# A hybrid RG-LRU and latent-attention trunk on one core: first weight chunks in one transfer, the first sums behind nine products, the last stage's sums on rounded parts

## The chip, the cores and the metric

The kernel runs on one core of a Trainium2 chip. The metric is device time in microseconds (us), the median of several runs; lower is better. The engines are TensorE (PE in the profile; PEld is its weight load), VectorE (DVE), ScalarE (ACT), GpSimd (POOL) and SyncE (SP), which here only issues transfers. Each engine works through its own list of instructions in the order in which they were written or scheduled, and they meet through semaphores.

## The reference

One sequence of 1024 positions with 1024 channels passes through a recurrent layer and then through an attention layer that reads one shared set of keys and values; a last RMS norm ends it.

```
h  = rms_norm(x, norm_a);  u = h @ w_in_a             # 1024 -> 2 x 1280
xb = causal_conv4(u[:, :1280]) ; gate = u[:, 1280:]
r, i = sigmoid(xb @ w_rg + b_rg), sigmoid(xb @ w_ig + b_ig)   # ten blocks of 128
a  = exp(-8 r softplus(-lam));  hs = scan(a, sqrt(1 - a^2) * i * xb)
x  = x + (hs * silu(gate)) @ w_out_a
ckv, k_rope from rms_norm(x, norm_kv) @ w_dkv;  k, v from rms_norm(ckv)
u  = rms_norm(x, norm_b) @ w_in_b;  q from rms_norm(u[:, :384]);  gate = u[:, 384:]
o  = causal attention of 8 heads (scores over 128 + 64 channels)
x  = x + (o * silu(gate)) @ w_out_b
out = rms_norm(x, final_norm)
```

## The kernel before

Channels lie on the 128 partitions and the 1024 positions along the free dimension; a tile of 512 positions is a half, `hs(0)` or `hs(1)`. A float32 number is kept as two parts in the type F32R: `hi`, a rounded copy that ScalarE makes, and `lo`, the rest, that VectorE makes by a subtraction (`hl`). A product is then three matmuls, hi by hi, hi by lo and lo by hi (`mm3`, lines 117 to 119).

**The beginning** (lines 286 to 365) is written out by hand for SP, ACT and DVE (`manual_schedule`); the lists of the other engines, and of all engines in the rest of the program, come from the scheduler. `warm` is nine matmuls on ones, whose results nobody reads. ACT issues the two transfers with the first 128 columns of the first x-branch chunk (`wx`) and gate chunk (`wg`) of the input weights. SP issues x (`xload`, tile by tile of 128 channels), with the remaining weights in between; ahead of them all it issues `vec`, a small table of gains and biases. `xsplit(k)` multiplies tile k of x by the norm's gain from `vec` and splits it into parts: ACT makes hi (L255), DVE lo (L256). The products start with the tiles k = 0 and 1, half by half (`first`, L325), and go on tile by tile (`products`), 96 matmuls for four accumulators `ps0`. In between ACT squares x (L278, L280) and DVE adds the squares into `accp` (L150, L152), since the norm's factor is applied to the results and not to x. The factor needs the sum over the partitions: `accp` is split into `ap`, and per half two matmuls with a matrix of ones (`onesr`, L362) give the sum; then `newton` makes the reciprocal square root with two ACT and two DVE instructions (L142 to L145) into `rb`.

**The loop over the ten chunks** `ct` follows. For a chunk, `conv` scales the products by `rb` (`byr`, L156), runs the convolution on DVE (L384) and splits the result `xc` (L85 on ACT, L86 on DVE); `rgig` multiplies the split result by the two gate matrices, six matmuls per half; and the products of the next chunk (`psn`, 48 matmuls on `wx`) and of its gate (`pg1` for chunk 1, 24 per half) stand ahead of `rgig` on PE. Weights of later chunks come as a raw float32 copy on SP and a rounded copy on POOL; DVE subtracts one from the other (L101). The softplus of `lam` is some 45 instructions of ten columns (`sp`), spread over DVE's list.

**The last stage** (lines 1043 to 1140) is the output product and the final norm. The first half of the positions goes tile by tile (eight tiles `dt`), the squares are added into `acc`; in the second half five tiles are 512 wide, and three are cut into two quarters, `qa` and `qb_`, of 256. Each norm sums its squares over the partitions with a float32 matmul on ones: `acc` at L1125, the first quarter's `acc2` at L1134, the second's at L1112 and L1113. `root` runs `newton`, and `multiplies` scales the tiles and issues the stores.

Of the kernel before, what the change touches and what calls it, by code (L numbers as in the profile page):

```python
# [10 lines left out]
F32R = mybir.dt.float32r  # L11
# [38 lines left out]
NWARM = 9  # L50
# [10 lines left out]
def trunk(tc, xT, wina, vecs, wgate, wouta, winc, wuk, wuv, wuq, wuqr, woutb, rope, outT):  # L61
# [69 lines left out]
    nc.sync.dma_start(out=vec, in_=vecs)  # L131
# [158 lines left out]
    with tc.manual_schedule(engines={_E.SP, _E.Activation, _E.DVE}):  # L290
        w0 = [Weights(wina[j][:, 0:4 * P], w) for j, w in ((0, wx), (NCT, wg))]
        for w in w0:
            w.load(0, 1, nc.scalar)
# [7 lines left out]
        xload(0, hs(0))  # L301
        xload(0, hs(1))
# [5 lines left out]
        xload(3)  # L308
        step(SPN[0])
        w0[0].split(0, 1)  # L310
        w0[1].split(0, 1)
        xsplit(0, hs(0))
# [43 lines left out]
        for h in range(2):  # L356
            hl(accp[:, hs(h)], *ap[h])
        for h in range(2):
            t1, t2 = tt(), tt()
            ps = pst()  # L360
            for i in range(2):
                T.matmul(out=ps, lhsT=onesr, rhs=ap[h][i], start=i == 0, stop=i == 1)  # L362
            newton(rb[:, hs(h)], ps, 1.0 / D, t1, t2)
# [79 lines left out]
    for ct in range(NCT):  # L443
# [12 lines left out]
        if ct + 1 < NCT:  # L456
            wg = wtile(wina[NCT + ct + 1], NKT, cast=True)
            psn = [pst(), pst()]
            for h in range(2):
                mmt(psn[h], wx, xs, hs(h))  # L460
            if ct == 0:
                pg1 = [pst(), pst()]
                for h in range(PG1):
                    mmt(pg1[h], wg, xs, hs(h))
            prev = (ct, rgig(ct, ws, xcs), gt)
            if ct == 0:
                for h in range(PG1, 2):
                    mmt(pg1[h], wg, xs, hs(h))
# [579 lines left out]

    def products(dt, c, po, k0=0, mid=None):
        k1 = NKT if mid is None else 5  # L1050
        mmt(po, wob[dt][k0:k1], ysb[k0:k1], c, first=k0 == 0, last=k1 == NKT)
        if mid:
            mid()
            mmt(po, wob[dt][k1:], ysb[k1:], c, first=False)
# [6 lines left out]
    for dt in range(NKT):  # L1061
# [14 lines left out]
        x2s.append(x2)  # L1076

# [42 lines left out]
    for dt in range(NWIDE):  # L1120
        tile2(dt, slice(0, HW))
        if dt == 1:

            ps = pm()
            T.matmul(out=ps, lhsT=onesd, rhs=acc, start=True, stop=True)  # L1125
# [4 lines left out]
    for dt in range(NWIDE, NKT):  # L1130
        tile2(dt, qa)
    def norm():
        ps = pm()[:, 0:HW // 2]
        T.matmul(out=ps, lhsT=onesd, rhs=acc2[:, qa], start=True, stop=True)  # L1134
        root(HW // 2, ps, acc2[:, qa])

    tile2(NWIDE, qb_, norm)
    multiplies(QUARTER, qa)
    for dt in range(NWIDE + 1, NKT):
        tile2(dt, qb_)  # L1140
    multiplies(FINAL, qb_)
# [54 lines left out]
```

## Time and profile before

| | |
|---|---|
| median of three runs | 866.5 us (866.46 to 866.98) |
| the profiled execution, its own time | 866.23 us |
| its span, first to last instruction | 864.5 us |
| mean granted clock of TensorE | 0.996 |
| busy, share of the span | PE 99%, DVE 76%, ACT 60%, POOL 9% |

The profiled execution's own time is 1.73 us above its span, and 0.27 us below the median. A busy share says how long an engine had an instruction in it; what an instruction waited for stands in the view of waits and, in brackets, at the end of a row of the timeline. Matmuls are pipelined: one lasts longer in the profile than the time from its start to that of the next.

### The profile page before, as it was taken

How to read it: one execution, taken by the hardware profiler on the slowest of the kernel's cores; microseconds unless marked ns; L12 is line 12 of the kernel's file. 1: busy time of each engine (PE TensorE's matmuls, PEld its weight loads, DVE VectorE, ACT ScalarE, POOL GpSimd, SP SyncE). 2: the span in 40 equal slices, each digit the busy share in tenths (PEclk: the TensorE clock that was granted, in tenths of full speed). 3: DMA queues.
4: the chain of work that ended last, by engine and by line, in shares of the span. 5: the costliest groups of instructions: out<-in, count | busy, mean ns of one | idle time of the engine just before them, and what ended most of it. 6: DMA issues, size and time to landing. Idle time of an engine off the chain costs nothing.

```text
span 864.5 us, 11922 instructions
## 1 busy us (share of the span) xinstructions
PE 851.9 (99%) x4206; PEld 721.7 (83%) x4206; DVE 659.5 (76%) x1216; ACT 519.9 (60%) x959; POOL 73.6 (9%) x143
## 2 busy tenths in 40 slices
PE   8999999999999999999999999999999999999995
PEld 6788888888888888888888889888998998888885
DVE  7888778777877773779998957887797887875254
ACT  8557787777688542699976555555565564431132
POOL 1000110110000110100312320000000000010000
PEclk9999999999999999999999999999999999999998
DMA  8333333333213445123545674122231323867022
GB/s 300 92 98 98 98 97 99 107 95 98 79 43 92 151 144 184 51 98 121 170 147 202 213 252 125 53 91 83 77 113 62 105 82 132 335 211 247 0 98 98
DMA packets 51052, 108.98 MB, mean 126 GB/s; under 512 B 6448, under 2 KB 15024, under 8 KB 50992
## 3 DMA queue, kind: packets, MB, share of 16 engines
q1 hardware_dynamic: 34928, 67.05, 23.7%
q0 software_dynamic: 15216, 40.51, 14.1%
q8 instruction: 33, 0.54, 0.3%
q10 hardware_dynamic: 848, 0.66, 0.2%
q14 instruction: 27, 0.22, 0.1%
HBM read 81.46 MB, written 26.21 MB: 125 GB/s over the span
## 4 chain that ended last, share of the span: by engine, by line
PE 95%; DVE 2%; issue 1%; DMA 1%; ACT 1%; SPq 0%; DVEq 0%
PE ps L118 18%; PE ps L117 18%; PE ps L119 18%; PE pm L119 6%; PE pm L117 6%; PE pm L118 6%; PE pm L922 4%; PE pm L938 2%; PE pm L939 2%; PE s L905 2%; PE s L903 2%; PE s L904 2%; PE s L906 2%; PE s L902 2%; PE pm L937 2%
## 5 line engine op out<-in xcount | busy, mean ns | idle before, releaser
L118 PE MATMUL ps<-pg,wh 128*128 128x512 f32 x664 | 258.7, 390 | 0.6 <-DVE pg L256 0.5
L119 PE MATMUL ps<-pg,wl 128*128 128x512 f32 x664 | 258.4, 389 | 0.0
L117 PE MATMUL ps<-pg,wh 128*128 128x512 f32 x664 | 257.8, 389 | 0.0
L118 PEld LDWEIGHTS ps<-pg,wh 128*128 128x128 f32 x664 | 124.6, 188 | 27.7 <-DVE pg L256 2.1
L117 PEld LDWEIGHTS ps<-pg,wh 128*128 128x128 f32 x664 | 124.6, 188 | 26.3 <-DVE tk L657 0.3
L119 PEld LDWEIGHTS ps<-pg,wl 128*128 128x128 f32 x664 | 124.6, 188 | 25.7
L85 ACT ACTIVATE pt<-pm 128x512 fp32r<-128x512 f32 (+2 forms) x96 | 44.4, 490 | 58.1 <-PE pm L922 54.8
L912 ACT ACTIVATE pg<-s,m 128x128 f32<-128x128 f32 (+3 forms) x64 | 47.5, 743 | 47.1 <-DVE m L909 40.7
L117 PE MATMUL pm<-pg,pg 128*128 128x512 f32 (+1 forms) x152 | 54.9, 361 | 0.0
L118 PE MATMUL pm<-pg,pg 128*128 128x512 f32 (+1 forms) x152 | 54.5, 359 | 0.0
L119 PE MATMUL pm<-pg,pg 128*128 128x512 f32 (+1 forms) x152 | 54.3, 357 | 0.0
L86 DVE TENSOR_TENSOR pt<-pm,pt 128x512 fp32r<-128x512 f32 (+2 forms) x96 | 50.5, 549 | 3.2 <-ACT pt L85 3.2
L909 DVE TENSOR_REDUCE m<-s 128x1 f32<-128x128 f32 (+3 forms) x64 | 48.1, 753 | 1.2
L384 DVE SCALAR_TENSOR_TENSOR t<-xb,vec,t 128x512 f32<-128x512 f32 x60 | 44.8, 746 | 0.4
L85 ACT ACTIVATE wh<-wr 128x512 fp32r<-128x512 f32 (+3 forms) x55 | 29.1, 531 | 25.4 <-PE ps L118 12.9
L85 ACT ACTIVATE pg<-pg 128x512 fp32r<-128x512 f32 x42 | 26.1, 631 | 29.5 <-DVE pg L438 18.1
L86 DVE TENSOR_TENSOR wl<-wr,wh 128x512 fp32r<-128x512 f32 (+3 forms) x55 | 30.6, 566 | 15.5 <-ACT wh L85 15.3
L119 PE MATMUL pm<-pg,wl 128*128 128x512 f32 x108 | 42.4, 392 | 0.0
L922 PE MATMUL pm<-ident,pg 128*128 128x128 f32 x288 | 42.3, 274 | 0.0
L118 PE MATMUL pm<-pg,wh 128*128 128x512 f32 x108 | 42.3, 392 | 0.0
L117 PE MATMUL pm<-pg,wh 128*128 128x512 f32 x108 | 42.2, 390 | 0.0
L902 PE MATMUL s<-pg,pg 128*128 128x512 f32 (+2 forms) x96 | 37.0, 386 | 0.4 <-ACT pg L912 0.4
(238 smaller groups left out, 1782.1 us busy)
## 6 DMA issues: line engine op xcount, KB each, us to landing
wr<-wina SPq DMA_DIRECT2D x38, 256.0 KB, 2.8
wh<-wina POOLq DMA_DIRECT2D x36, 256.0 KB, 2.9
wa<-winc SPq DMA_DIRECT2D x24, 256.0 KB, 3.2
ysd<-pg POOLq DMA_DIRECT2D x12, 512.0 KB, 3.0
pg<-ysd SPq DMA_DIRECT2D x12, 512.0 KB, 10.6
wr<-wouta SPq DMA_DIRECT2D x16, 256.0 KB, 2.7
t<-xT SPq DMA_DIRECT2D x16, 256.0 KB, 3.6
x1d<-t POOLq DMA_DIRECT2D x16, 256.0 KB, 2.5
```

The costliest lines, as they stand in the source:

```text
L85: A.activation(out=hi, in_=src, func=AF.Copy)
L86: V.tensor_tensor(out=lo, in0=src, in1=f(hi), op=ALU.subtract)
L117: T.matmul(out=ps, lhsT=w[0], rhs=r[0], start=first, stop=False, skip_group_check=more)
L118: T.matmul(out=ps, lhsT=w[0], rhs=r[1], start=False, stop=False, skip_group_check=more)
L119: T.matmul(out=ps, lhsT=w[1], rhs=r[0], start=False, stop=last, skip_group_check=more)
L384: V.scalar_tensor_tensor(out=xc, in0=xb[:, j:j + HW], scalar=cwv[j], in1=xc, op0=ALU.mult, op1=ALU.add)
L902: T.matmul(out=sc[:, c], lhsT=q[0][:, ql], rhs=k[0][:, c], start=True, stop=False)
L903: T.matmul(out=sc[:, c], lhsT=q[0][:, ql], rhs=k[1][:, c], start=False, stop=False)
L904: T.matmul(out=sc[:, c], lhsT=q[1][:, ql], rhs=k[0][:, c], start=False, stop=False)
L909: V.tensor_reduce(out=m, in_=sc, axis=AX.X, op=ALU.max, negate=True)
L912: A.activation(out=p_[:, 0:nk], in_=sc, func=AF.Exp, bias=m, accum_out=l)
L922: T.transpose(out=ps[:, (b - b0) * P:(b - b0 + 1) * P], in_=p_[:, b * P:(b + 1) * P], identity=ident)
```

## The change

Five edits:

- The two first weight chunks come in one transfer on ACT's queue, of 128 partitions by 2 by 128 columns, into one tile `raw0`; the rounding of both (`hl`) reads from there and stands ahead of the first five instructions of the softplus.
- SP issues the first half of x tile 0 ahead of `vec`. `warm` has eight matmuls instead of nine.
- Nine products of the next chunk (`psn0`: tiles k = 0 to 2 of the first half) stand ahead of the first sums (L362) in the program; the loop's first pass then takes k = 3 to 7 for this half.
- The sums of `acc` and of the first quarter's `acc2` in the last stage are made of the two rounded parts, as the first sums are: `sumparts` splits, and `total` is two F32R matmuls in place of one float32 matmul. The one of `acc2` stands behind seven of the eight k of its tile, instead of five.
- The last of the first quarter's four scalings with its store stands behind the next tile's product.

```diff
-NWARM = 9
+NWARM = 8
...
     vec = con.tile([P, NVEC], F32, name="vec")
-    nc.sync.dma_start(out=vec, in_=vecs)
...
-        for w in w0:
-            w.load(0, 1, nc.scalar)
+
+        raw0 = tt()[:, 0:2 * P]
+        nc.scalar.dma_start(out=raw0.rearrange("p (j c) -> p j c", c=P), in_=wina[0:NCT + 1:NCT, :, 0:P].rearrange("j p c -> p j c"))
...
         xload(0, hs(0))
+        nc.sync.dma_start(out=vec, in_=vecs)
         xload(0, hs(1))
...
+        for i, w in enumerate(w0):
+            hl(raw0[:, i * P:(i + 1) * P], w.hi[:, 0:P], w.lo[:, 0:P])
+        xsplit(0, hs(0))
         step(SPN[0])
-        w0[0].split(0, 1)
-        w0[1].split(0, 1)
-        xsplit(0, hs(0))
         xsplit(0, hs(1))
...
             hl(accp[:, hs(h)], *ap[h])
+        psn0 = pst()
+        mmt(psn0, wx[:3], xs[:3], hs(0), last=False)
         for h in range(2):
             t1, t2 = tt(), tt()
...
-            psn = [pst(), pst()]
+            psn = [psn0 if ct == 0 else pst(), pst()]
             for h in range(2):
-                mmt(psn[h], wx, xs, hs(h))
+                k0 = 3 if (ct, h) == (0, 0) else 0
+                mmt(psn[h], wx[k0:], xs[k0:], hs(h), first=k0 == 0)
...
+    def sumparts(a):
+
+        n = a.shape[-1]
+        p_ = td.tile([P, n], F32R, tag="t1", name=nm("t1")), td.tile([P, n], F32R, tag="t2", name=nm("t2"))
+        hl(a, *p_)
+        return p_
+
+    def total(ps, p_):
+
+        for i in range(2):
+            T.matmul(out=ps, lhsT=onesr, rhs=p_[i], start=i == 0, stop=i == 1)
+
     def products(dt, c, po, k0=0, mid=None):
-        k1 = NKT if mid is None else 5
+        k1 = NKT if mid is None else 7
...
         x2s.append(x2)
+    ap = sumparts(acc)
...
-            T.matmul(out=ps, lhsT=onesd, rhs=acc, start=True, stop=True)
+            total(ps, ap)
             root(HW, ps, acc)
...
         tile2(dt, qa)
+    ap = sumparts(acc2[:, qa])
+
     def norm():
         ps = pm()[:, 0:HW // 2]
-        T.matmul(out=ps, lhsT=onesd, rhs=acc2[:, qa], start=True, stop=True)
+        total(ps, ap)
         root(HW // 2, ps, acc2[:, qa])

     tile2(NWIDE, qb_, norm)
-    multiplies(QUARTER, qa)
+    multiplies(QUARTER[:3], qa)
     for dt in range(NWIDE + 1, NKT):
         tile2(dt, qb_)
+        if dt == NWIDE + 1:
+            multiplies(QUARTER[3:], qa)
```

How this changes the engines' lists is not all in the diff, since the scheduler orders anew. Three places matter below. In the changed kernel the lines of `newton` are L141 to L144 (one less than before), `byr` is L155, the sums L365 and the convolution L387.

The first place is PE's list at the first sums, just behind the last product for `ps0`. Before, the tiles `t_337` to `t_340` are the parts of `accp`, and `ps_441` is the next chunk's first half:

```order
L119 MATMUL ps_153<-pg_299,wl_181 128x512
L362 MATMUL ps_347<-t_337,onesr 128x512
L362 MATMUL ps_356<-t_339,onesr 128x512
L362 MATMUL ps_347<-t_338,onesr 128x512
L117 MATMUL ps_441<-pg_144,wh_326 128x512
L118 MATMUL ps_441<-pg_145,wh_326 128x512
L362 MATMUL ps_356<-t_340,onesr 128x512
```

In the change `ps_344` is the next chunk's first half; of its nine products the last three are shown with what follows:

```order
L117 MATMUL ps_344<-pg_203,wh_325 128x512
L118 MATMUL ps_344<-pg_204,wh_325 128x512
L119 MATMUL ps_344<-pg_203,wl_326 128x512
L365 MATMUL ps_356<-t_336,onesr 128x512
L365 MATMUL ps_356<-t_337,onesr 128x512
L365 MATMUL ps_365<-t_338,onesr 128x512
L365 MATMUL ps_365<-t_339,onesr 128x512
L117 MATMUL ps_344<-pg_222,wh_325 128x512
```

The four matmuls for the sums now stand together, nine products later; the rest of the list up to `rgig` is the same.

The second place is DVE's list behind the splitting of `accp`. Before, `wl_431` and `wl_437` are the second parts of the next gate weights (each waits for two transfers), and L144 and L145 are the two DVE steps of `newton`, first for half 0 and then for half 1:

```order
L101 TENSOR_TENSOR wl_431<-wr_429,wh_430 128x512
L144 SCALAR_TENSOR_TENSOR t_346<-ps_347,t_346 128x512
L101 TENSOR_TENSOR wl_437<-wr_435,wh_436 128x512
L145 SCALAR_TENSOR_TENSOR accp<-t_346,t_345 128x512
L144 SCALAR_TENSOR_TENSOR t_355<-ps_356,t_355 128x512
L156 SCALAR_TENSOR_TENSOR xb_400<-ps_150,accp 128x512
L145 SCALAR_TENSOR_TENSOR accp<-t_355,t_354 128x512
```

and in the change:

```order
L101 TENSOR_TENSOR wl_440<-wr_438,wh_439 128x512
L101 TENSOR_TENSOR wl_446<-wr_444,wh_445 128x512
L143 SCALAR_TENSOR_TENSOR t_355<-ps_356,t_355 128x512
L144 SCALAR_TENSOR_TENSOR accp<-t_355,t_354 128x512
L143 SCALAR_TENSOR_TENSOR t_364<-ps_365,t_364 128x512
L155 SCALAR_TENSOR_TENSOR xb_409<-ps_149,accp 128x512
L144 SCALAR_TENSOR_TENSOR accp<-t_364,t_363 128x512
```

Both weight subtractions now stand ahead of `newton`.

The third place is DVE's list at the end of chunk 0's convolution, some 25 rows on. Before, `t_415` is the convolved second half, `wl_581` weights of chunk 2, and L86 makes the second part `t_421` that `rgig` reads:

```order
L384 SCALAR_TENSOR_TENSOR t_415<-xb_412,vec,t_415 128x512
L210 SCALAR_TENSOR_TENSOR sp_132<-sp_132,sp_131 128x10
L384 SCALAR_TENSOR_TENSOR t_415<-xb_412,vec,t_415 128x512
L210 SCALAR_TENSOR_TENSOR sp_132<-sp_132,sp_131 128x10
L101 TENSOR_TENSOR wl_581<-wr_579,wh_580 128x512
L210 SCALAR_TENSOR_TENSOR sp_132<-sp_132,sp_131 128x10
L86 TENSOR_TENSOR t_421<-t_415,t_420 128x512
```

In the change these are `t_424`, `wl_580` and `t_430`:

```order
L101 TENSOR_TENSOR wl_580<-wr_578,wh_579 128x512
L209 SCALAR_TENSOR_TENSOR sp_139<-sp_139,sp_138 128x10
L387 SCALAR_TENSOR_TENSOR t_424<-xb_421,vec,t_424 128x512
L209 SCALAR_TENSOR_TENSOR sp_139<-sp_139,sp_138 128x10
L387 SCALAR_TENSOR_TENSOR t_424<-xb_421,vec,t_424 128x512
L209 SCALAR_TENSOR_TENSOR sp_139<-sp_139,sp_138 128x10
L211 TENSOR_SCALAR sp_137<-sp_137 128x10
L381 COPY xb_596<-xb_584 128x3
L155 SCALAR_TENSOR_TENSOR xb_596<-ps_450,accp 128x512
L213 CAST spi<-sp_137 128x10
L86 TENSOR_TENSOR t_430<-t_424,t_429 128x512
```

The weights' subtraction moved ahead of the last two convolution steps, and a scaling of the next chunk (L155, 512 columns) with four small instructions moved in ahead of L86.

## Rows read from the trace of the kernel before

**Rows 1.** Waits of PE: line, releaser, total us, times, longest.

```profile
PE ps L325 <- ACT pg L255: 0.9, 1, 0.9
PE ps L362 <- DVE t L86: 0.5, 1, 0.5
```

**Rows 2.** Timeline, beginning: start, length, engine, line, instruction [idle before, releaser].

```profile
4.70 0.31 ACT L85 ACTIVATE wh<-wr 128x128 fp32r<-128x128 f32 x1 [1.33 <-DMA wr<-wina]
...
5.67 0.73 PE L325 MATMUL ps<-pg,wh 128*128 128x512 f32 x2 [0.93 <-ACT pg L255]
...
9.66 1.15 ACT L255 ACTIVATE pg<-pg,vec 128x1024 fp32r<-128x1024 f32 x1 [0.56 <-DMA pg<-xT]
...
12.74 1.23 DVE L152 TENSOR_TENSOR accp<-accp,pg 128x1024 f32<-128x1024 f32 x1 [0.61 <-ACT pg L280]
...
21.08 0.19 PEld L118 LDWEIGHTS ps<-pg,wh 128*128 128x128 f32 x1 [0.20 <-DVE pg L256]
```

**Rows 3.** Windows, beginning: stretch, length, busy us per engine, clock, DMA share, GB/s.

```profile
1.25:4.00 2.75, 2.75 (x13) 2.75 (x14) 1.22 (x12) 1.69 (x3) 0.44 (x2) 1.00 0.77 198
4.00:4.50 0.50, 0.50 (x7) 0.50 (x5) 0.11 (x1) 0.00 (x0) 0.00 (x0) 1.00 1.06 344
1.75:3.50 1.75, 1.75 (x10) 1.75 (x10) 0.56 (x5) 1.61 (x3) 0.00 (x0) 1.00 0.91 210
3.50:9.25 5.75, 4.82 (x25) 3.92 (x25) 4.13 (x10) 3.94 (x7) 0.00 (x0) 1.00 1.02 358
```

**Rows 4.** Timeline at the first sums, PE and DVE.

```profile
29.14 0.76 PE L362 MATMUL ps<-t,onesr 128*128 128x512 f32 x2
...
29.61 1.29 DVE L86 TENSOR_TENSOR t<-accp,t 128x512 fp32r<-128x512 f32 x2
...
30.36 0.50 PE L362 MATMUL ps<-t,onesr 128*128 128x512 f32 x1 [0.45 <-DVE t L86]
...
31.39 0.39 PE L119 MATMUL ps<-pg,wl 128*128 128x512 f32 x1
```

**Rows 5.** Timeline, DVE and ACT from newton to the end of chunk 0's convolution.

```profile
32.67 0.63 ACT L143 ACTIVATE t<-t 128x512 f32<-128x512 f32 x1
...
33.44 0.69 DVE L101 TENSOR_TENSOR wl<-wr,wh 128x512 fp32r<-128x512 f32 x1 [2.54 <-DMA wr<-wina]
...
34.05 0.68 DVE L144 SCALAR_TENSOR_TENSOR t<-ps,t 128x512 f32<-128x512 f32 x1
...
34.89 0.69 DVE L101 TENSOR_TENSOR wl<-wr,wh 128x512 fp32r<-128x512 f32 x1 [0.15 <-DMA wr<-wina]
...
37.89 0.17 DVE L196 CAST sp<-spi 128x10 f32<-128x10 int32 x1
...
45.95 0.75 DVE L384 SCALAR_TENSOR_TENSOR t<-xb,vec,t 128x512 f32<-128x512 f32 x1
46.69 0.69 DVE L101 TENSOR_TENSOR wl<-wr,wh 128x512 fp32r<-128x512 f32 x1
47.40 0.69 DVE L86 TENSOR_TENSOR t<-t,t 128x512 fp32r<-128x512 f32 x1
```

**Rows 6.** The same stretch: ACT's copy of the second half, and its second product.

```profile
46.73 0.64 ACT L85 ACTIVATE t<-t 128x512 fp32r<-128x512 f32 x1 [3.07 <-DVE t L384]
...
48.86 0.39 PE L118 MATMUL ps<-t,wh 128*128 128x512 f32 x1
```

**Rows 7.** Timeline, last stage: the two float32 sums and the instruction behind each.

```profile
819.14 1.02 PE L1125 MATMUL pm<-acc,onesd 128*128 128x512 f32 x2
...
820.23 0.39 PE L118 MATMUL pm<-pg,pg 128*128 128x512 f32 x1
...
846.11 0.43 DVE L152 TENSOR_TENSOR acc<-acc,sq 128x256 f32<-128x256 f32 x1 [0.48 <-ACT sq L1109]
...
846.80 0.59 PE L1134 MATMUL pm<-acc,onesd 128*128 128x256 f32 x2
...
847.35 0.28 PE L118 MATMUL pm<-pg,pg 128*128 128x256 f32 x1
```

## The prediction

> **What bounds the kernel now.** I read the page's busy shares first (PE 99%, in the table above), then the waits of PE, then the timeline at each place that the diff touches, and last the windows of the beginning. PE is the bound almost everywhere: of its waits on other engines only a handful are recorded, and two of the longer ones lie where the change works, 0.9 us ahead of the first product and 0.5 us at the first sums [rows 1]. So whatever PE loses or saves between the first sums and its last product arrives in the time in full. The exception is the beginning. There the reader should follow who waits last: ACT stands idle for 0.56 us until x tile 2 has landed and splits it from 9.66 [rows 2]; its work from there sets DVE's start on the squares at 12.74, after 0.61 us idle; and PE still waits for DVE's second parts at 21.08 [rows 2]. PE begins at 5.67, and the distance to its first sum at 29.14 [rows 4] is 23.5 us for 96 products of 0.227 us, that is 21.8 us of work (the 0.227 us is worked out from 31.39 to 48.86, which are 77 starts, 17.47 us [rows 4, 6]). 1.7 us of that stretch is therefore waiting, and the place of the first product is not what ends it. The landing of x tile 2 is.
>
> **The one transfer, and x ahead of the vectors.** ACT's first part now waits for the joint transfer instead of the second of two, which it got at 4.70 [rows 2]. It may land sooner (one issue less in front of it) or later (twice the bytes, beside x). In both cases PE has 1.7 us in hand, and ACT has its 0.56 us ahead of tile 2, so the first product is free to move. By itself it is worth nothing. What counts is whether x tile 2 lands sooner. The bytes are the same, but now 256 KB of x lead the queue instead of the small table. From 1.75 to 3.50 the transfers ran at 210 GB/s, later at 358 [rows 3]. If the early stretch ran at the later rate, (358 - 210) x 1.75 / 358 = 0.72 us would be gained; if nothing changes, 0. A ramp from nothing remains in either order, so I take 0.3 us, a little below the middle. Against it stands the Trainium skill, "DMA: Bandwidth & Descriptors", section "Issuing engines are not separate DMA queues": transfers of all queues interleave on the same sixteen engines, so that another queue or order saves issue time only. By this rule alone the gain is 0 and the sum below ends 0.3 us higher; the low rate at the start says that the engines were not full yet, which is why I don't take it. The moved softplus steps (five of some 0.17 us on DVE, like the CAST in [rows 5]) fit into DVE's idle time: from 3.50 to 9.25 it is busy for 4.13 of 5.75 us [rows 3], and it waits for ACT ahead of 12.74. **-0.3 us (0 to -0.72).** One `warm` less ends PE's run-up some 0.15 us sooner (two starts at 0.07 [rows 3]) and costs nothing unless the clock falls (below).
>
> **Nine products ahead of the first sums.** Now PE starts the first L362 at 29.14 and the product L119 that follows the four of them at 31.39 [rows 4]. In these 2.25 us it starts six matmuls, which need 6 x 0.227 = 1.36 us. The rest, **0.89 us**, is the wait for DVE's second parts of `accp`, the last of which is done at 29.61 + 1.29 = 30.90 [rows 4]. With nine products in between, the sums begin at 29.14 + 9 x 0.227 = 31.18, behind 30.90. The wait is gone.
>
> What is late next: the sums come out about 1.1 us later, and the scheduler has moved things behind them. DVE works through its list in order. Before, L144 for half 0 stood between two weight subtractions; its ACT input was ready at 32.67 + 0.63 = 33.30, yet it ran at 34.05, right behind an L101 that waited 2.54 us for a weight transfer; the second L101 came at 34.89, again at the end of a transfer [rows 5]. Now both L101 stand ahead. Starts of independent 512-column instructions lie 0.60 us apart (33.44, 34.05). So in the old time scale: first `newton` step at 34.89 + 0.60 = 35.49; the second needs its result (0.68, and 0.12 until it is taken): 36.29; three more instructions at 0.60 each, then the CAST at 38.69. It was at 37.89 [rows 5]. DVE's whole convolution is 0.80 us late.
>
> From there to the end of chunk 0's convolution the list has the same instructions up to the third convolution step of half 1, plus the L101 that used to follow it (46.69 to 47.40 with the small one behind it, 0.71 us) and one ten-column step (some 0.1). That step, 45.95 before [rows 5], comes at 45.95 + 0.80 + 0.71 + 0.1 = 47.56 and ends 0.75 later, 48.31. ACT's copy takes 0.64 [rows 6]: 48.97. DVE meanwhile has a scaling of 0.60 and small ones, some 0.8 us together, so that L86 starts near 49.13 (it was 47.40) and ends at 49.82. PE's product L118 reads it. It ran at 48.86 [rows 6], with the part ready at 47.40 + 0.69 = 48.09 [rows 5], a margin of 0.77. With the 0.89 us saved PE stands there at 47.97 and waits until 49.87: **1.90 us**, in two pieces, for ACT's copy and for DVE's rest. A restart costs some 0.1 us more (the matmul at 30.36, after a wait, lasts 0.50 instead of 0.39 [rows 4]). Behind this product stand all of PE's others; nothing else on PE can fill in. Against the old time this place is 1.90 + 0.10 - 0.89 = **1.1 us later**. Bounds: if DVE's list were no later than before, the product would be ready at 48.09, a wait of 0.1 and a gain of 0.8; if the ten-column steps cost 0.17 us each all along, it would be 0.4 worse than I count. The list is fixed and its durations are known, so I take the count. Behind `rgig` PE is later against DVE than before, so no further wait should appear in the chunks.
>
> **The last stage.** The float32 sum at L1125 and one product take PE from 819.14 to 820.23, 1.09 us [rows 7]; without the product's 0.227, 0.86. Two F32R matmuls take 0.45: -0.41 us. The one at L1134 takes 846.80 to 847.35, less one product of 256 columns (half of 0.227 by columns; I use 0.12), 0.43; two of 0.12 take 0.24: -0.19 us. The parts of `acc` are hidden: behind them PE still has the products of two 512-wide tiles, 48 x 0.227 = 10.9 us, ahead of the sum. Those of `acc2` are not: it is complete at 846.11 + 0.43 = 846.54 [rows 7], ACT's copy and DVE's rest take 0.43 each and ACT has 0.08 of a scaling left, so the second part is ready near 847.5; seven products instead of five put its matmul at 846.80 + 6 x 0.12 + 0.12 = 847.64. No wait, by 0.1 us. The fourth scaling (some 0.6 us on DVE), moved behind the next tile, ends some 0.7 us ahead of the last tile's addition by my count of DVE's list (a tile of a quarter takes PE 24 x 0.12 = 2.9 us, the three scalings, additions and squares in it about 2.6). **-0.6 us (-0.3 if the part comes 0.3 later than I count).**
>
> **Sum.** 866.23 (the profiled execution's own time, 1.73 above its span) - 0.3 + 1.1 - 0.6 = 866.4. That execution was 0.27 below the median of the runs, so **866.7 us**: what the sums give is taken back at `rgig`.
>
> **Rivals.** *The sums' gain is kept*: the weight transfers, which end DVE's 2.54 us of idle time, land sooner, or DVE catches up, so that the part is ready in time. Then 866.5 - 0.3 - 0.89 - 0.6 = 864.7 us, faster. For it speaks that those transfers, issued earlier by what the beginning gains, may also run faster; against it that the second L101 would have to come 0.76 us sooner only to restore the old state, and the L155 and L101 in front of L86 are in the list whatever lands. *The clock falls in the new wait*, the rival on the slower side: PE ran its warm-up matmuls on the lower of its two levels at first, 13 starts in the 2.75 us to 4.00 and 7 in the next 0.5 us [rows 3], though the granted clock reads 1.00. If the two-piece wait at `rgig` threw it back for such a stretch, half of some 2.8 us of work is lost, 1.4 us: 868.1 us, and slower outright if the beginning gains nothing. Against it: after 0.93 us idle the first pair of products took 0.73 us [rows 2], where two starts at half the rate are 0.45 apart and the pair would last 0.9 or more. The Trainium skill, "TensorE: Matmul & The Clock Gate", Part 1, makes the low level the state of an idle array; no row here shows a wait of this length, so it decides nothing yet. *The joint transfer lands late*: ACT is busy for 3.94 us from 3.50 to 9.25 [rows 3], to which the first of the two roundings comes, 0.3; it must be done by 9.66, so if it begins later than 5.4, what lies beyond counts. A landing at 6.4 would make it 867.7 us. Its 128 KB next to 256 KB of x speak against.
>
> **How the numbers follow.** Forecast 0.78 (866.0 to 867.3, from the bounds of the beginning and the count of DVE's list); gain kept in full 0.10, half of it past the bound; clock 0.06, half of it; late transfer 0.06. A measurement of this kernel tells a change of about 0.2%, 1.7 us, from none: below 864.8 or above 868.2. Faster 0.09, same 0.82, slower 0.09. The range 865.0 to 867.7 leaves out most of the first and second rival.
>
> **What would show it.** PE's waits: the one on DVE's `t` at the sums gone, two new ones at the products of `t` and `wh` of chunk 0, 1.2 and 0.7 us, the releasers ACT L85 and DVE L86. The timeline: both L101 ahead of `newton`, L86 of the second half near 49.5 (49.8 less the beginning's 0.3). The split of x tile 2 at about 9.4; the first product near 5.0. In the last stage two matmuls 0.45 and 0.24 us long, without idle time. I am wrong if no wait shows at `rgig`, if x tile 2 lands over 0.7 us sooner or later than 9.66, or if PE waits in a later chunk.

## The result, and the profile after

The change makes the kernel slower: 868.65 us (median of 11 runs, 867.91 to 871.24) against 866.77 (11 runs, 866.40 to 867.82) on the same chip, ratio 1.0025, 95% interval 1.0016 to 1.0035 (the ratio is taken over all runs; the medians lie 1.88 us apart). The forecast was 866.7, its range 865.0 to 867.7. The profiled execution took 868.58 us, its span is 866.8 (before 864.5), so 2.3 us have to be found in it. Before, the profiled execution was 0.54 us below the median of the runs, and here it is 0.07 below, so some 0.5 of the 2.3 belongs to which executions were profiled.

The waits of PE come first (line, releaser, total us, times, longest):

```profile
PE ps L117 <- ACT t L85: 1.1, 1, 1.1
...
PE ps L117 <- ACT ps L641: 0.5, 1, 0.5
...
PE ps L118 <- DVE t L86: 0.3, 1, 0.3
```

The wait for DVE at the first sums [rows 1] is gone. The two waits at `rgig`, on ACT L85 and DVE L86, are those that were forecast. The one on ACT L641 was not: it lies in the attention layer's projections, some 380 us behind `rgig` and far ahead of the last stage. The timeline gives each its place (start, length, engine, line, instruction, [idle before, releaser]):

```profile
10.15 1.15 ACT L254 ACTIVATE pg<-pg,vec 128x1024 fp32r<-128x1024 f32 x1 [0.98 <-DMA pg<-xT]
...
31.70 1.08 PE L365 MATMUL ps<-t,onesr 128*128 128x512 f32 x4
...
32.62 0.39 PE L117 MATMUL ps<-pg,wh 128*128 128x512 f32 x1
...
33.70 0.69 DVE L101 TENSOR_TENSOR wl<-wr,wh 128x512 fp32r<-128x512 f32 x1 [2.30 <-DMA wr<-wina]
35.45 0.69 DVE L101 TENSOR_TENSOR wl<-wr,wh 128x512 fp32r<-128x512 f32 x1 [1.05 <-DMA wr<-wina]
36.05 0.68 DVE L143 SCALAR_TENSOR_TENSOR t<-ps,t 128x512 f32<-128x512 f32 x1
...
48.82 0.63 ACT L85 ACTIVATE t<-t 128x512 fp32r<-128x512 f32 x1 [3.87 <-DVE t L387]
...
49.60 0.69 DVE L86 TENSOR_TENSOR t<-t,t 128x512 fp32r<-128x512 f32 x1
...
50.34 0.50 PE L118 MATMUL ps<-t,wh 128*128 128x512 f32 x1 [0.33 <-DVE t L86]
...
372.48 2.49 DVE L151 TENSOR_TENSOR acc<-acc,t 128x512 f32<-128x512 f32 x4
...
375.00 0.60 ACT L641 ACTIVATE v<-ps 128x512 f32<-128x512 f32 x1 [0.51 <-DVE acc L151]
...
420.75 0.60 ACT L656 ACTIVATE pg<-ps 128x512 f32<-128x512 f32 x1 [0.91 <-DMA kvd<-pg]
...
428.64 0.39 PE L119 MATMUL ps<-pg,wl 128*128 128x512 f32 x1
429.52 0.50 PE L117 MATMUL ps<-pg,wh 128*128 128x512 f32 x1 [0.49 <-ACT ps L641]
...
821.63 0.62 PE L1063 MATMUL pm<-t,onesr 128*128 128x512 f32 x2
...
822.32 0.40 PE L118 MATMUL pm<-pg,pg 128*128 128x512 f32 x1
...
849.58 0.40 PE L1063 MATMUL pm<-t,onesr 128*128 128x256 f32 x2
...
849.93 0.28 PE L118 MATMUL pm<-pg,pg 128*128 128x256 f32 x1
...
858.66 0.42 DVE L143 SCALAR_TENSOR_TENSOR t<-pm,t 128x256 f32<-128x256 f32 x1 [2.10 <-ACT t L142]
859.54 0.42 DVE L144 SCALAR_TENSOR_TENSOR acc<-t,t 128x256 f32<-128x256 f32 x1 [0.46 <-DVE t L143]
```

The places in the kernel before that no earlier row shows:

```profile
370.82 2.50 DVE L152 TENSOR_TENSOR acc<-acc,t 128x512 f32<-128x512 f32 x4
...
372.75 0.58 ACT L637 ACTIVATE v<-ps 128x512 f32<-128x512 f32 x1
...
418.24 0.60 ACT L652 ACTIVATE pg<-ps 128x512 f32<-128x512 f32 x1 [0.66 <-DMA kvd<-pg]
...
427.22 0.39 PE L117 MATMUL ps<-pg,wh 128*128 128x512 f32 x1
...
856.79 0.43 DVE L144 SCALAR_TENSOR_TENSOR t<-pm,t 128x256 f32<-128x256 f32 x1 [2.10 <-ACT t L143]
857.32 0.43 DVE L145 SCALAR_TENSOR_TENSOR acc<-t,t 128x256 f32<-128x256 f32 x1
```

How the 2.3 us add up, each as the difference of the same instruction in both (plus is later than before). x tile 2 is split at 10.15 instead of 9.66: +0.5. At the first sums PE has done seven matmuls more when it starts L117 at 32.62 than it had done at 31.39 [rows 4]; 32.62 - 7 x 0.227 = 31.03, so PE stands at -0.36: the sums gave 0.86. L118 behind `rgig` comes at 50.34 instead of 48.86 [rows 6]; the products behind it start slowly at first (0.34 and 0.24 us apart instead of 0.23), and from then on PE stands at +1.65: `rgig` took 2.01. At 427 PE waits again. Its next product would have started at 428.64 + 0.23 = 428.87, which is +1.65 against 427.22; it starts at 429.52, and with the restart PE stands at +2.43: **0.78 lost in a place far behind the change**. The last stage gives back 0.56 (+1.87 at 858.66). Between `newton`'s last two DVE steps lie 0.88 us instead of 0.53: +2.22. The last 0.1 is in the final stores.

### The profile page after: what moved, and what is told of

Read it like the earlier page. It is cut to its first block, busy times and chain, and to the rows that moved or that the text cites. A ratio compares the mean times of both kernels' runs of the same rounds, so it can differ in the third digit from the quotient of the medians.

```text
span 866.8 us, 11921 instructions
## 1 busy us (share of the span) xinstructions
PE 852.3 (98%) x4204; PEld 721.4 (83%) x4204; DVE 660.1 (76%) x1218; ACT 520.9 (60%) x961; POOL 73.3 (8%) x143
## 4 chain that ended last, share of the span: by engine, by line
PE 91%; DVE 3%; DMA 2%; issue 2%; ACT 1%; POOL 0%; DVEq 0%; POOLq 0%; ACTq 0%
PE ps L118 16%; PE ps L117 16%; PE ps L119 16%; PE pm L119 6%; PE pm L118 6%; PE pm L117 6%; PE pm L926 4%; PE pm L942 2%; PE pm L943 2%; PE s L908 2%; PE s L909 2%; PE s L907 2%; PE s L910 2%; PE s L906 2%; PE pm L941 2%
## 5 line engine op out<-in xcount | busy, mean ns | idle before, releaser
L118 PE MATMUL ps<-pg,wh 128*128 128x512 f32 x664 | 258.8, 390 | 0.9 <-DVE pg L255 0.8
L117 PE MATMUL ps<-pg,wh 128*128 128x512 f32 x664 | 258.0, 390 | 0.5 <-ACT ps L641 0.5
L118 PEld LDWEIGHTS ps<-pg,wh 128*128 128x128 f32 x664 | 124.6, 188 | 28.2 <-DVE pg L255 2.4
L117 PEld LDWEIGHTS ps<-pg,wh 128*128 128x128 f32 x664 | 124.5, 188 | 27.3 <-ACT ps L641 0.9
L85 ACT ACTIVATE pt<-pm 128x512 fp32r<-128x512 f32 (+2 forms) x96 | 44.3, 490 | 58.2 <-PE pm L926 54.9
L118 PE MATMUL pm<-pg,pg 128*128 128x512 f32 (+1 forms) x152 | 54.5, 359 | 0.0
L117 PE MATMUL pm<-pg,pg 128*128 128x512 f32 (+1 forms) x152 | 54.2, 357 | 0.0
L86 DVE TENSOR_TENSOR pt<-pm,pt 128x512 fp32r<-128x512 f32 (+2 forms) x96 | 50.5, 549 | 3.3 <-ACT pt L85 3.2
L387 DVE SCALAR_TENSOR_TENSOR t<-xb,vec,t 128x512 f32<-128x512 f32 x60 | 44.8, 746 | 0.3
L85 ACT ACTIVATE pg<-pg 128x512 fp32r<-128x512 f32 x42 | 26.1, 630 | 31.4 <-DVE pg L441 18.9
L85 ACT ACTIVATE wh<-wr 128x512 fp32r<-128x512 f32 (+2 forms) x53 | 28.4, 538 | 23.7 <-PE ps L118 12.4
L118 PE MATMUL pm<-pg,wh 128*128 128x512 f32 x108 | 42.3, 392 | 0.0
L117 PE MATMUL pm<-pg,wh 128*128 128x512 f32 x108 | 42.2, 391 | 0.0
L86 DVE TENSOR_TENSOR wl<-wr,wh 128x512 fp32r<-128x512 f32 (+2 forms) x53 | 30.0, 576 | 13.9 <-ACT wh L85 13.7
```

What stands on the lines that cost most here:

```text
L85: A.activation(out=hi, in_=src, func=AF.Copy)
L86: V.tensor_tensor(out=lo, in0=src, in1=f(hi), op=ALU.subtract)
L117: T.matmul(out=ps, lhsT=w[0], rhs=r[0], start=first, stop=False, skip_group_check=more)
L118: T.matmul(out=ps, lhsT=w[0], rhs=r[1], start=False, stop=False, skip_group_check=more)
L387: V.scalar_tensor_tensor(out=xc, in0=xb[:, j:j + HW], scalar=cwv[j], in1=xc, op0=ALU.mult, op1=ALU.add)
```

## The experiments

Each is compared with the kernel before on the same chip (866.76 to 866.93).

**Each part alone.** e1 is the kernel before with these lines, and nothing else of the change:

```
+        psn0 = pst()
+        mmt(psn0, wx[:3], xs[:3], hs(0), last=False)
...
+                k0 = 3 if (ct, h) == (0, 0) else 0
+                mmt(psn[h], wx[k0:], xs[k0:], hs(h), first=k0 == 0)
```

> The kernel before with the nine products ahead of the first sums alone. Theory (the wait at rgig): the 0.86 us wait at the sums goes, two waits on ACT L85 and DVE L86 at chunk 0's rgig come, 1.9 us together, so the time is 1.0 to 1.1 us above before (ratio 1.0012). Rival (the loss of the change lies elsewhere, the sums' gain is kept): 0.9 us below before (ratio 0.9990).

869.54, ratio 1.0026 (1.0017 to 1.0035). The nine products alone cost as much as the whole change: by the medians more, by the ratios the two cannot be told apart. PE gains 0.88 at the sums, stands at +1.27 behind `rgig`, and waits in the projections again, 0.4 us near 394 and 1.06 at 427:

```profile
377.28 0.69 ACT L536 ACTIVATE wa<-wa,vec 128x128 f32<-128x128 f32 x2 [1.12 <-DMA wa<-winc]
...
429.88 0.50 PE L117 MATMUL ps<-pg,wh 128*128 128x512 f32 x1 [0.77 <-ACT ps L640]
```

So the late wait belongs to this part. The path differs a little: here ACT waits for a weight tile `wa`, whose transfer SP issued at 374.62 instead of 369.18; in the changed kernel it waits to write `v`.

e2 is the last stage alone (`sumparts`, `total`, seven products, the fourth scaling behind the next tile):

```
+            total(ps, ap)
-            T.matmul(out=ps, lhsT=onesd, rhs=acc, start=True, stop=True)
```

> The kernel before with the edits of the last stage alone. Theory: two sums 0.6 us shorter on PE and nothing else, 0.6 us below before (ratio 0.9993). Rival (the moved scaling or the new parts lengthen the closing chain on DVE, where the change shows a step 0.35 us later): 0.2 us below before or the same.

865.97, ratio 0.9989 (0.9980 to 0.9998): faster than the kernel before.

**What makes the late wait.** The recurrent layer takes its tiles `t` from a ring of 14, which is closed when that layer ends. The tiles of the attention stage (`wa`, `v2`, `cc`, `tk`) lie in the memory that the ring held, so the first writer of such a tile must wait for the last reader of the ring tile under it. Two first guesses were that any shift of the ring by one tile, or the joint transfer's tile in it, brings the wait:

```
+        spare = tt()                          # e3: before, one more ring tile
+        V.memset(spare[:, 0:1], 0.0)
-        raw0 = tt()[:, 0:2 * P]               # e4: changed kernel
+        raw0 = accp[:, 0:2 * P]
```

> The kernel before with one more tile taken from the pool of fourteen ahead of the beginning, written with one column of zeros and never read. Theory (the shift of the pool's rotation): the first weights of the attention projections wait for another tile's last reader, some 4 us later than 369 us, ACT and DVE lose 0.6 us, and PE waits near 427 us: 0.5 to 0.8 us above before. Rival (that wait comes from the later PE or from chance): no difference, no wait near 427.

> The changed kernel with the joint transfer's tile laid into accp, which is free then, in place of a tile of the rotating pool. Theory (rotation): the weights' transfers near 369 us issue as before, no wait of PE near 427, 0.7 us below the changed kernel. Rival (chance, or PE's lag): as the changed kernel, a wait near 427 as there.

e3: 866.75, ratio 0.9999 (0.9990 to 1.0007), no new wait. e4: 868.86, ratio 1.0021 (1.0012 to 1.0030), the wait stays, 0.6 on ACT L641. Both guesses fell in this form. (In e4's built program the ring lies as in e1, so this edit exchanged one bad place, described next, for another.)

The addresses in the built programs gave a sharper one. Near 371 us DVE makes the last four additions to `acc1` and then one L86; each reads a ring tile. In the kernel before, the fourth one's tile begins at byte 196832, under a `tk` tile that is written later. In the changed kernel it begins at 212192, exactly where `v2` lies (in the rows it is named `v`); and `v` is ACT's next instruction. In e1 it overlaps `wa`. The nine products change the order of the lists in chunk 0, and from that chunk's first L86 on many of the ring's tiles have another place (93 of 198 in e1). That they do because tiles now come free in another order is read off the programs, not tested. e5 puts the overlap of the changed kernel into the kernel before, without any part of the change; e6 uses the same spares to lift it in e1:

```
+        for _ in range(6):
+            V.memset(tt()[:, 0:1], 0.0)
```

> Edit: the kernel before, plus six spare tiles of the ring of 14 at the start; no other part of the change. Read from the built programs: where a ring tile lies in memory decides what the first tiles of the attention stage, which reuse that memory, wait for. With six spares the fourth of the four last additions to acc1 (DVE, 370.82 to 373.3 in the profile before) reads a tile under v2, which ACT must write at about 372.7; in the kernel before that tile lies under tk, which is written later. The changed kernel has the same overlap with v2 (ACT idles 0.51 there <- DVE acc). Theory 'place in memory': ACT waits about 0.5 us at v2, and PE about 0.3 to 0.9 us at 427, with no wait at rgig: 867.2 to 867.6. Rival 'PE's delay at rgig is needed for the second wait': no wait at 427, time as before, 866.5 to 867.0.

> Edit: the kernel before with the nine products alone, plus six spare ring tiles at the start. With these the last additions' tiles lie under tk tiles, and no longer under the first weight tile wa (run e1: SP's first transfer of wa issued at 374.62 instead of 369.18). Theory 'place in memory': the wait at rgig stays (PE +1.2 against the kernel before, as in e1), the waits at 393 and 427 are gone: 867.8 to 868.2, against 869.54 of e1. Rival 'the lateness at rgig causes the later waits': as e1, 869.2 to 869.8.

e5, 867.50, ratio 1.0006 (0.9998 to 1.0015); the time alone is within the uncertainty, the rows are not:

```profile
374.22 0.60 ACT L639 ACTIVATE v<-ps 128x512 f32<-128x512 f32 x1 [0.50 <-DVE acc L152]
...
428.87 0.50 PE L117 MATMUL ps<-pg,wh 128*128 128x512 f32 x1 [0.60 <-ACT ps L639]
```

The wait is there with nothing late at `rgig` (PE goes from +0.89 to +1.78 at 427; the 0.89 is this execution's beginning). e6 missed: 869.00, ratio 1.0028 (1.0017 to 1.0039), and PE still waits at 427:

```profile
375.60 1.67 ACT L694 ACTIVATE tk<-acc 128x512 f32<-128x512 f32 x3 [0.63 <-DVE wl L86]
...
429.63 0.50 PE L117 MATMUL ps<-pg,wh 128*128 128x512 f32 x1 [0.58 <-ACT ps L642]
```

The row names what I had overlooked: the additions' tiles were moved away, but the first `tk` now lay under the tile of the L86 behind them. e9 takes the changed kernel and four spares. The tile of the fourth addition then lies under a later `tk` and that of the L86 under a later `cc`; only the third addition's lies under the first `tk`, and it has been read by then:

> Edit: the changed kernel plus four spare ring tiles at the start, each with a memset of one column. Read from the built program: no tile of the attention stage that ACT or SP needs early lies any longer under a tile that DVE still reads then; e6 and e7 had overlooked the first tk tile, which lay under the tile of the L86 behind the additions (ACT idles 0.63 there <- DVE wl L86). Theory 'place in memory': ACT idles nowhere between 373 and 377, PE has no step at 427 (0.83 in the changed kernel): about 0.8 less. It also has five more DVE instructions, see the next run: the gap between newton's last two DVE steps at the very end 0.53 instead of 0.88. Together 867.4 to 867.7 against 868.65. Rival 'PE's later place at rgig makes the wait': step at 427 stays, 868.2 to 868.6.

867.45, ratio 1.0010 (1.0001 to 1.0019), as the first theory said and 1.2 us under the changed kernel. ACT writes `v` at once, the step of PE at 427 is 0.17 instead of 0.78, though PE comes as late from `rgig` as in the changed kernel (50.32 at L118). In the built programs ACT's write of `v` waits for the fourth addition in the changed kernel and in e5, and for nothing in e9:

```profile
374.35 0.58 ACT L643 ACTIVATE v<-ps 128x512 f32<-128x512 f32 x1
...
857.90 0.42 DVE L143 SCALAR_TENSOR_TENSOR t<-pm,t 128x256 f32<-128x256 f32 x1 [2.10 <-ACT t L142]
858.43 0.43 DVE L144 SCALAR_TENSOR_TENSOR acc<-t,t 128x256 f32<-128x256 f32 x1
```

A smaller term goes with it. In every profile ACT stands still near 420 until a transfer `kvd` has landed: 0.66 us before, 0.91 in the changed kernel, 0.90 in e9. In the profiles without a harmful place the step at 427 follows this wait: 0.02 or none where it is 0.54 to 0.73, and 0.15 to 0.38 where it is 0.87 to 1.06 (e8, e9, e11, e14, e15). So of the changed kernel's 0.78 some 0.6 belongs to the place in memory and some 0.2 to this transfer; what delays it was not tested.

**The gap at the end** is 0.53 again in e9. e10 changes only the number of DVE's instructions (`tiny` is written twice):

> Edit: the changed kernel with one more DVE memset (tiny, written twice) and the same ring. In the runs so far the last newton's two DVE steps start 0.53 us apart (before, e2, e3, e5, e6, e7) or 0.88 apart (after, e1, e4, e8); the programs of the second kind have 1484 instructions on DVE, waits included, with these two as numbers 1471 and 1472, the others 1485 or more. Theory 'place in the DVE program': with 1485 the gap is 0.53 again, 0.35 less: 868.3, and the step at 427 stays at 0.8. Rival 'the beginning or the data decides': 0.88 again, 868.65.

```profile
374.86 0.60 ACT L642 ACTIVATE v<-ps 128x512 f32<-128x512 f32 x1 [0.51 <-DVE acc L152]
...
858.35 0.42 DVE L144 SCALAR_TENSOR_TENSOR t<-pm,t 128x256 f32<-128x256 f32 x1 [2.10 <-ACT t L143]
858.88 0.42 DVE L145 SCALAR_TENSOR_TENSOR acc<-t,t 128x256 f32<-128x256 f32 x1
```

The gap is 0.53 and the wait at `v` stays, so the two are separate. 867.95, ratio 1.0014 (1.0005 to 1.0023); that is 0.7 under the changed kernel where 0.35 was expected, and the rest is not explained.

**The wait at `rgig`.** e7 uses six products instead of nine, with e6's spares. With six, DVE's list has `newton`'s first step between the two L101 again:

```
-        mmt(psn0, wx[:3], xs[:3], hs(0), last=False)
+        mmt(psn0, wx[:2], xs[:2], hs(0), last=False)
```

> Edit: six products ahead of the first sums instead of nine (6 x 0.23 = 1.38 us, still more than the wait of 0.89), with the six spare ring tiles; beginning and last stage as before. With six, the written order of DVE keeps newton's first step between the two L101, as before the change, instead of behind both. Theory 'the order on DVE makes the wait at rgig': no wait over 0.2 us at rgig, the gain of 0.85 at the sums is kept, no wait at 393 or 427: 865.9 to 866.3. Rival 'any gain at the sums is lost at rgig, since DVE's chain sets that time': PE waits 0.8 at rgig and the time is as before, 866.6 to 867.0.

867.98, ratio 1.0014 (1.0005 to 1.0022): a miss. PE gains 0.89 at the sums and loses 1.28 at `rgig` and 1.32 more at 427, where e6's place of the first `tk` is still at work and the wait for `kvd` is the longest of all, 1.30:

```profile
34.87 0.68 DVE L144 SCALAR_TENSOR_TENSOR t<-ps,t 128x512 f32<-128x512 f32 x1
...
46.32 0.69 DVE L101 TENSOR_TENSOR wl<-wr,wh 128x512 fp32r<-128x512 f32 x1
...
48.68 0.69 DVE L156 SCALAR_TENSOR_TENSOR xb<-ps,accp 128x512 f32<-128x512 f32 x1
...
49.26 0.51 PE L117 MATMUL ps<-t,wh 128*128 128x512 f32 x1 [0.38 <-ACT t L85]
...
49.35 0.69 DVE L86 TENSOR_TENSOR t<-t,t 128x512 fp32r<-128x512 f32 x1
...
50.09 0.50 PE L118 MATMUL ps<-t,wh 128*128 128x512 f32 x1 [0.33 <-DVE t L86]
...
429.77 0.50 PE L117 MATMUL ps<-pg,wh 128*128 128x512 f32 x1 [1.03 <-ACT ps L642]
```

The order at `newton` is not the only thing that moved. In this execution x tile 2 is split 0.92 later than before (10.58). Less that, `newton`'s first step is back at 33.95 (before 34.05), and yet the L86 comes at 48.43, 1.0 later than before [rows 5]; in the changed kernel, less its 0.5, it is 1.7 later. So of DVE's 1.7 us some 0.7 come from the order at `newton` and some 1.0 from the order at the end of the convolution, which e7 does not undo: a later L101 still stands ahead of two of the convolution's steps (in the kernel before, behind the third of them), and the scaling L156 of chunk 1 ahead of the L86 that PE waits for (before, behind it). e11 keeps nine products and takes the two L101 at `newton` off DVE altogether, with five harmless spares:

```
-                V.tensor_tensor(out=lo, in0=raw, in1=f(hi), op=ALU.subtract)
+                (sub or V).tensor_tensor(out=lo, in0=raw, in1=f(hi), op=ALU.subtract)
...
+            wg = wtile(..., cast=True, sub=G if ct == 0 else None)
```

> Edit: the kernel before with the nine products alone, the two L101 subtractions of chunk 1's second weights moved from DVE to GpSimd, and five spare ring tiles (harmless places as in e9). Theory 'the two L101 ahead of newton make the wait at rgig': newton starts on DVE some 1.9 us earlier than in e1 (35.72 there), no wait over 0.2 us at rgig, the 0.86 at the sums is kept, no step at 393 or 427: 865.8 to 866.2. Rival 'the rest of DVE's chain (the chunk 2 weights and the evacuation of chunk 1 that now stand ahead of the second half) is enough': PE waits 0.3 to 0.9 at rgig, 866.3 to 866.9. A second rival: GpSimd takes over 3 us for each subtraction and PE waits for wl of chunk 1 at about 43: slower than 867.

> Edit: the same as e11 plus the last stage as changed (e2: 865.97 against 866.76, so -0.8). If the two add up: 865.0 to 865.3, the fastest version so far. Rival: one of the parts is taken back elsewhere, 865.8 or more.

e11: 866.43, ratio 0.9994 (0.9985 to 1.0003); e12, 865.95, ratio 0.9989 (0.9980 to 0.9998). In e11:

```profile
32.69 1.29 POOL L101 TENSOR_TENSOR wl<-wr,wh 128x512 fp32r<-128x512 f32 x1 [2.74 <-DMA wr<-wina]
...
33.18 0.69 DVE L144 SCALAR_TENSOR_TENSOR t<-ps,t 128x512 f32<-128x512 f32 x1 [2.26 <-ACT t L143]
...
47.49 0.69 DVE L86 TENSOR_TENSOR t<-t,t 128x512 fp32r<-128x512 f32 x1
...
48.23 0.50 PE L118 MATMUL ps<-t,wh 128*128 128x512 f32 x1
```

`newton` starts 2.5 us earlier than in e1 (35.72), the L86 1.8 us earlier (49.26), and of the wait at `rgig` 0.3 us are left (PE goes from -0.84 to -0.52). So it is DVE's lateness that PE waits for. Which order makes it late is not told by e11: without the two L101, `newton` starts 0.9 earlier than even in the kernel before (34.05), and that covers for the order at the end of the convolution, which is the changed one here too. Both times came out above what was expected, by 0.2 and 0.65 from its upper ends; in e11 PE loses 0.38 at 427, behind a wait of 0.94 for `kvd`. Against e2 the nine products bring nothing that the medians show (865.95 and 865.97), though e12's span is the shortest of all, 863.3 against 864.0.

**The beginning.** e8 is the changed kernel without the nine products; e13 is the beginning alone, with the ring as in e3 and two memsets against the gap; e14 gives it nine warm products; e15 puts the vectors ahead of x again; e16 is the kernel before with eight warm products:

```
-NWARM = 8                                             # e14
+NWARM = 9
+        nc.sync.dma_start(out=vec, in_=vecs)          # e15: this line first
         xload(0, hs(0))
```

> Edit: the changed kernel without the nine products: beginning and last stage as changed. Its ring tiles lie as in e3 (no harmful place). If the parts add up, this run less e2 (865.97) is the beginning's own price. Theory from the profile of after (x tile 2 split at 10.15 instead of 9.66): the beginning costs 0.3 to 0.5 us, so 866.3 to 866.5. Rival, the forecast's term of -0.3: 865.7. The spread of the runs is expected as wide as that of the changed kernel (over 2 us) if the beginning causes it, under 1.5 us otherwise.

> Edit: the kernel before with the changed beginning alone (joint transfer of both first weight chunks, x ahead of vec, 8 warm products), a harmless place of the ring as in e3, and two more DVE memsets so that the gap of e10 at the end is 0.53 as before. From e8 less e2 (0.0002 + 0.0011 of 866.8 = 1.1) less 0.35 for the gap: theory 'the beginning costs': 867.3 to 867.6, x tile 2 split near 10.2 instead of 9.7. The forecast's term of -0.3: 866.5.

> Edit: as e13 with nine warm products on PE instead of eight. Two of the five profiles with the changed beginning (e4, e10) have a spell between 6 and 9.5 in which products start 0.43 us apart instead of 0.23, one with the old beginning has a few (e11). Theory 'one warm product less makes the spell': none here, 0.3 to 0.6 less than e13. Rival 'the order of the transfers alone': as e13 within 0.3.

> Edit: as e13 with the vectors again ahead of x on SP's queue. In the stretch 4.0 to 5.4 the changed beginning moves 171 to 252 GB/s, the old one 307 to 368. Theory 'vec between two parts of x holds x up': that stretch above 300 GB/s again, x tile 2 split near 9.7, 866.7. Rival 'the joint transfer (ACT issues one instead of two) is what is late': as e13.

> Edit: the kernel before with eight warm products instead of nine, nothing else. Theory 'one warm product less makes the spell of 0.43 us': 867.1 to 867.6 and such a spell in the profile. Rival: 866.6 to 867.0, no spell.

e8: 866.90, ratio 1.0002 (0.9993 to 1.0011). Its runs span 1.6 us (866.29 to 867.87), the changed kernel's 3.3; under 1.5 or over 2 was expected, so what widens them stays open. e13: 867.16, ratio 1.0004 (0.9995 to 1.0012). e14: 867.30, ratio 1.0004 (0.9995 to 1.0013). e15: 867.22, ratio 1.0002 (0.9993 to 1.0011). e16: 866.84, ratio 0.9998 (0.9989 to 1.0007). No interval excludes no change; the three medians with the joint transfer stand 0.3 to 0.5 above the kernel before, the one without it does not. The theories of e14, e15 and e16 fell: with a ninth warm product the time is no lower than e13's, with the vectors first again x tile 2 is split at 10.09 as in e13, and with eight warm products alone there is neither a loss nor a spell of slow products (the last section has that spell). The windows (stretch, length, PE busy us (count), granted clock, DMA share, GB/s), here of before, the changed kernel, e13, e14, e15 and e16:

```profile
4.00:5.40 1.40, 0.74 (x7) 1.00 1.01 324
```

```profile
4.00:5.40 1.40, 0.82 (x5) 1.00 0.95 207
```

```profile
4.00:5.40 1.40, 0.87 (x5) 1.00 1.07 192
...
6.50:9.50 3.00, 3.00 (x9) 1.00 1.02 394
```

```profile
4.00:5.40 1.40, 1.30 (x8) 1.00 1.24 176
```

```profile
4.00:5.40 1.40, 1.17 (x6) 1.00 1.04 211
```

```profile
4.00:5.40 1.40, 0.71 (x5) 1.00 1.07 339
```

With the joint transfer the DMA engines move 176 to 211 GB/s from 4.00 to 5.40, about as busy as before; without it 324 and 339. Over all profiles it is 171 to 252 in the eight with the joint transfer and 307 to 368 in the ten with two. The hole goes with the joint transfer, not with the order of `vec` nor with the ninth warm product. That it is what makes x tile 2 late is argued, not shown: in the eight profiles with the joint transfer the split begins at 9.65 to 10.98 (middle 10.13), in the ten with two transfers at 9.43 to 11.13 (middle 9.80). PE's place at the first sums follows this split, as the forecast had it: in 14 of the 17 other profiles its distance from before is that of the split within 0.1 us, and in e6, e10 and e13 it is 0.3 to 0.4 more. But with two transfers the split already moves by 1.7 us from profile to profile, so the +0.5 of the changed kernel's profile is one execution's figure and not the price of the change.

## Why the prediction was wrong

**The first sums**: right. 0.89 us was forecast to go, 0.86 went.

**`rgig`**: right in mechanism and size. Forecast 1.90 of wait and 0.10 of restart in two pieces, for ACT's copy and DVE's rest; measured 2.01 in total, in two pieces on these releasers. The L86 was expected at 49.13 less 0.3 and came at 49.60; less the 0.5 by which this execution began late, that is 49.10, as counted. Both parts of the count hold: by e7 some 0.7 us come from the two L101 ahead of `newton` (counted 0.80) and some 1.0 from the end of the convolution (counted 0.93).

**"Behind `rgig` PE is later against DVE than before, so no further wait should appear in the chunks"**: this is the step that failed, by 0.78 us. The conclusion was drawn from the order of the lists, which in the projections is the same as before, and left out a second thing that the scheduler sets: where each ring tile lies. A tile at another address makes another instruction wait for the same reader. From the 0.51 us at `v` on, ACT is 2.25 us later than before (375.00 against 372.75) and PE only 1.65. ACT has no idle time to speak of until it waits for `kvd` at 420, so it catches up nothing, and at 427 PE needs what ACT writes. e5 shows the wait without the nine products, e9 the nine products with 0.17 of it left.

**The beginning**: the wrong sign in the profile, +0.5 instead of -0.3; alone, +0.3 with an interval that includes none. The step that failed is the estimate that the early stretch would run at the later rate. The low rate at the start was read as a sign that the engines were not full, but [rows 3] has them busy for 0.91 of that stretch, against 1.02 later, so there was little left to fill. In the changed kernel the stretch from 1.75 to 3.50 does run at 229 GB/s instead of 210, but the one from 4.00 to 5.40 at 207 instead of 324. The rule that stood against my value was nearer: by the Trainium skill, "DMA: Bandwidth & Descriptors", section "Issuing engines are not separate DMA queues", transfers that several engines start run on the same sixteen DMA engines, and spreading them saves issue time only. That another order on one queue gains nothing either is my own step from it, and the runs bear it out: e13 and e15 differ in this order alone, and both split x tile 2 at 10.09. A small reading was wrong as well: the 7 in [rows 3] counts every matmul that the window touches, and the fast warm products start 0.11 us apart, not 0.07.

**The last stage**: right. By the rows it saves 0.40 and 0.20 (821.63 to 822.32 less one product of 0.227 is 0.46 against 0.86 [rows 7]; 849.58 to 849.93 less 0.12 is 0.23 against 0.43), as forecast, and no wait took its place. In the medians e2 is 0.8 faster.

**Not in the sum at all**: 0.35 us at the end, which e10 traces to the count of DVE's instructions.

The three that were missed, 0.78, 0.8 (from -0.3 to +0.5) and 0.35, make 1.9, about the difference between forecast and result, 1.95. With e13's +0.3 in place of the one execution's +0.5 they make 1.7; that the sum comes so near is in part chance. Of the rivals, none describes what happened: the gain was not kept, the restart at `rgig` ran at 0.34 and then 0.24 us per product, not at half rate, and the joint transfer was not late (ACT rounds from it at 4.30, where the second of two came at 4.70 [rows 2]); x tile 2 set the beginning.

## What to carry to other kernels

Where tiles come from rings and closed pools, an edit that reorders one engine's list also moves later tiles to other addresses; compare the addresses at each pool's border, and ask which reader ends last under the first tiles written behind it. A few spare tiles can cost or give back as much as the edit itself (four gave back 1.2 us here, with the gap at the end), so an edit that "does nothing" to a stage has to be compared in more than one such layout before its own price is told. And a gain ahead of a place where another engine's list sets the time is worth only the margin there: 0.77 us, less what the reordering costs that engine.

## What the hardware showed that I had not expected

The last two steps of `newton` start 0.53 us apart in 14 of the programs here and 0.88 apart in four (the changed kernel, e1, e4, e8). In these four, and only these, DVE's list has 1484 instructions, waits included, and the second step is number 1472, counted from 0, behind the first (1470) and a wait (1471); in the others it is number 1473 to 1477. (The expectation of e10 meant the wait and the second step by its two numbers.) With one memset more the gap is 0.53. So the place in the list goes with the gap in all 18 programs, and e10 moves it on purpose; what DVE does in the 0.35 us was not measured.

At the beginning, products can start 0.43 us apart instead of 0.23 for some 3 us: e13 has nine in the 3.00 us from 6.50, all of it busy, where the kernel before has 15. 512 columns in 0.43 us are 1.2 per ns, so I take it for the lower of the two levels, 1.2 GHz; the granted clock in the row reads 1.00 and does not show it. Ahead of it PE had run its warm products and was idle for a part of the stretch from 4.00 (busy 0.87 of 1.40). e4 and e10 have the same spell, and e11 (with the old beginning) and e15 have two or three such starts near 6. In these five the first two products start 0.59 us apart, in the 13 others 0.33 to 0.44. The time from the start of the last warm product to that of the first real one does not tell them apart (0.65 to 1.02 us in the five, 0.52 to 1.54 in the others), and neither does the count of warm products (eight in e4, e10, e13 and e15, nine in e11). PE makes up for more than half of it where it would have waited for x: in e13 it is late by 1.6 at 9.4 and by 0.7 at 19.5.
